# VectorE instead of GpSimd makes the low parts of 72 dense weight pieces in a two-layer decoder trunk

## The chip, the cores and the metric

The kernel runs as one program on one core of a Trainium2 chip. Its time is the device time of one execution in microseconds (us). The engines are named as in the profile: PE is TensorE (PEld its weight loads), DVE is VectorE, ACT is ScalarE, POOL is GpSimd, SP issues most transfers. All of them run side by side, each through its own list of instructions in order, and wait for one another by semaphores.

## The reference

272 tokens (16 meta tokens and 256 of the input) of width 1024 pass two layers. Each layer projects the stream by one matrix of 8192 columns, runs a gated linear recurrence (8 heads) and a causal depthwise convolution of width 31 beside each other, merges both, and ends in a dense SwiGLU (layer 0) or a mixture of 8 experts, two per token (layer 1). Cut to what matters:

```
proj = h @ w_in[l]                                  # Q F I OG CV CG GA GB, 1024 columns each
o = hgrn2_recurrence(proj Q, proj F, proj I)        # per head, chunked over time
y_rec  = (rms_norm(o) * hg_norm_g * silu(proj OG)) @ w_hg_out
u = (proj CV) * sigmoid(proj CG)
y = conv over 31 tokens of u, per channel, + conv_b
y_conv = silu(layer_norm(y)) @ w_conv_out           # mean and variance over all channels
h = layer_norm(ALPHA * h + (sigmoid(proj GA) * y_rec + sigmoid(proj GB) * y_conv) @ w_out)
h = layer_norm(ALPHA * h + swiglu or mixture of experts)
```

## The kernel before

**Split products.** A dense product is made of three TensorE products in the fast float format fp32r: high weight by high input, high weight by low input, low weight by high input. The weights come from memory in pieces of 128 x 1024 numbers (`raw`). For each piece ScalarE copies the high part (`whi`), and then VectorE or GpSimd subtracts it from the piece, which gives the low part (`wlo`); `split` does both. `lo_pool(i)` says which engine makes the low part of piece i: GpSimd for the pieces 0 and 2 to 92 and for 156 to 235, VectorE for the others. A layer's mixer takes 88 pieces (0 to 87 and 156 to 243), the dense SwiGLU of layer 0 the 68 between. `SPLIT` = 6 pieces may stand ready.

**Stages.** The mixer goes through its columns in blocks of 256, two pieces each, in the order CG0 CV0, CG1 CV1, then F I Q of heads 0 to 3, CG2 CV2 CG3 CV3, then F I Q of heads 4 to 7, then the four blocks of OG and the four of GB. Behind those comes the product with `w_conv_out`, whose first two blocks are done together (`gemm_both`, L423) and whose input is the finished, normalised convolution, `yc_hi` and `yc_lo`. The pieces 20 to 55 (and 176 to 211 in layer 1) are those of CG2 up to GB.

**What runs beside.** The convolution (`conv`) is a chain of VectorE instructions: 8 blocks of 128 channels with 31 taps each, 248 taps a layer, each 128x272 (128x256 in layer 1), its input in SBUF and its running sum `st` in PSUM. Then come the sums over channels (`sums`), their TensorE reduction (L650, L651), the inverse deviation (`rstd`, ScalarE) and two passes of VectorE over all blocks. The recurrence (`attention`) runs once for heads 0 to 3 and once for heads 4 to 7: at each span of 1, 2, 4 up to 256 tokens TensorE makes products (L820, L826, L870, L877; bank `ca`), and VectorE multiplies decays into `q`, `k`, `kt` and `c` and copies the products under a mask into `att`. Both are Python generators. Behind each half of a block of weights `gemm` calls `prep`, which writes the splits of the coming pieces, and then `pump`, which takes one step of the recurrence and then as many taps as fit:

```
self.t_dve = max(self.t_dve, self.t_pe - 6.0)
while self.fill and self.t_dve < self.t_pe - 2.0:
    try:
        next(self.fill[0])
```

`t_pe` and `t_dve` are the planner's own counts of TensorE and VectorE work. Every VectorE instruction given out through `self.V` (a `Priced`) adds 0.1 us and its elements per partition / 960 us to `t_dve`; one given out through `nc.gpsimd` adds nothing. Behind the last GB block `finish_fill` writes whatever the convolution has left, with its norm. The order of every engine is fixed by this when the program is built.

Of the kernel before, what the change touches and what calls it, by code (L numbers as in the profile page):

```python
# [48 lines left out]
RAW, SPLIT, DENSE = 6, 6, 244  # L49
# [79 lines left out]
class Trunk:  # L129
# [226 lines left out]
    def lo_pool(self, i):  # L356
        if i >= DENSE:
            return DENSE + 4 <= i < DENSE + 6
        return i != 1 and i < 93 or 156 <= i < DENSE - 8

    def take(self, n):
# [1628 lines left out]
```

## Time and profile before

| | |
|---|---|
| runs | 1883.96, 1885.85, 1886.17 us; median 1885.85 |
| the profiled execution | 1887.53 us, span of the profile 1885.8 us |
| PE busy | 1811.1 us, 96% of the span |
| DVE, ACT, POOL busy | 1068.0 (57%), 824.1 (44%), 483.9 us (26%) |
| GpSimd's low parts | 173 instructions, 418.8 us |
| granted TensorE clock, mean | 0.984 |

Shares over the whole span mix stages. The mixer of layer 0 reaches from about 20 to 360 us, that of layer 1 from about 575 to 925 us, and the mixture of experts fills the time from about 940 us on.

### The profile page before, as it was taken

To read this page: it belongs to the slowest core of one execution; us is meant where nothing else is said; L and a number is where in the kernel's file an instruction comes from. 1 tells how busy PE (TensorE), PEld (TensorE's weight loads), DVE (VectorE), ACT (ScalarE), POOL (GpSimd) and SP (SyncE) were. 2 spreads that over 40 slices of the span, in tenths; PEclk is the share of its full clock that TensorE was granted. 3 is DMA by queue.
4 is the path that set the end of the run, shared out by engine and by line. 5 is a ranking of instruction groups with operands and counts; after the bars stand their busy time and mean duration, and the time that the engine had idled before them with its cause. 6 is when DMAs were issued, how large, how long until landed. Compare 5 with 4: busy or idle time off the path is not lost. (4 is left out here: it accounts for less than half of the span.)

```text
span 1885.8 us, 30795 instructions
## 1 busy us (share of the span) xinstructions
PE 1811.1 (96%) x11577; PEld 1400.9 (74%) x11577; DVE 1068.0 (57%) x1646; ACT 824.1 (44%) x1256; POOL 483.9 (26%) x258
## 2 busy tenths in 40 slices
PE   8989999899999998899899999999999999999996
PEld 7989899799999998899888888887443333433342
DVE  6999834865556899725799998986001001100112
ACT  4635545454446544555487877875001011111111
POOL 6857656500007856654200000000000000000000
PEclk8999999999999999999899999999999999999998
DMA  6534344455554534345689799999999999999995
GB/s 210 172 109 147 100 124 137 132 179 171 180 169 147 169 119 123 112 127 165 221 295 385 277 358 345 360 347 382 393 394 394 394 394 391 395 394 391 378 391 217
DMA packets 284162, 484.88 MB, mean 257 GB/s; under 512 B 15042, under 2 KB 139842, under 8 KB 284006
## 3 DMA queue, kind: packets, MB, share of 16 engines
q1 hardware_dynamic: 283654, 481.75, 72.3%
q8 instruction: 93, 1.52, 0.3%
q0 software_dynamic: 320, 1.08, 0.2%
q14 instruction: 63, 0.52, 0.1%
q10 hardware_dynamic: 32, 0.01, 0.0%
HBM read 481.73 MB, written 1.05 MB: 256 GB/s over the span
## 5 line engine op out<-in xcount | busy, mean ns | idle before, releaser
L126 ACT ACTIVATE whi<-raw 128x1024 fp32r<-128x1024 f32 (+1 forms) x498 | 518.9, 1050 | 113.5 <-PE mm L1565 41.4
L228 POOL TENSOR_TENSOR wlo<-raw,whi 128x1024 fp32r<-128x1024 f32 (+1 forms) x173 | 418.8, 2440 | 375.2 <-ACT whi L126 359.1
L104 DVE TENSOR_TENSOR wlo<-raw,whi 128x1024 fp32r<-128x1024 f32 (+1 forms) x323 | 386.7, 1217 | 92.8 <-ACT whi L126 80.2
L396 PE MATMUL mm<-h_hi,whi 128*128 128x272 f32 (+1 forms) x1280 | 377.7, 295 | 0.9 <-ACT tmp L126 0.9
L398 PE MATMUL mm<-h_hi,wlo 128*128 128x272 f32 (+1 forms) x1280 | 370.4, 289 | 0.0
L397 PE MATMUL mm<-h_lo,whi 128*128 128x272 f32 (+1 forms) x1280 | 369.0, 288 | 0.0
L396 PEld LDWEIGHTS mm<-h_hi,whi 128*128 128x128 f32 x1280 | 243.8, 191 | 2.6 <-ACT tmp L126 1.2
L1900 POOL TENSOR_TENSOR res<-res,four 128x256 f32<-128x256 f32 x2 | 2.3, 1143 | 943.3 <-ACT res L126 943.3
L397 PEld LDWEIGHTS mm<-h_lo,whi 128*128 128x128 f32 x1280 | 244.1, 191 | 0.1
L398 PEld LDWEIGHTS mm<-h_hi,wlo 128*128 128x128 f32 x1280 | 243.4, 190 | 0.0
L1628 PE MATMUL mm<-raw,xg 128*32 128x512 f32 (+1 forms) x896 | 200.6, 604 | 2.3 <-DMA raw<-in_moe_w_gate_dram 1.4
L104 DVE SCALAR_TENSOR_TENSOR st<-wide,cw,st 128x272 f32<-128x272 f32 (+1 forms) x480 | 194.4, 487 | 0.0
L126 ACT ACTIVATE tmp<-mm 128x512 f32<-128x512 f32 (+2 forms) x108 | 54.7, 509 | 245.5 <-PE mm L1628 165.6
L1564 PE MATMUL mm<-whi,xg 128*128 128x512 f32 x336 | 132.7, 395 | 0.0
L1628 PEld LDWEIGHTS mm<-raw,xg 128*32 128x32 f32 (+1 forms) x896 | 57.7, 129 | 99.3 <-issue 70.5
L1565 PE MATMUL mm<-whi,xg 128*128 128x512 f32 x336 | 131.3, 391 | 0.0
L1566 PE MATMUL mm<-wlo,xg 128*128 128x512 f32 x336 | 131.2, 391 | 0.0
L1717 DVE TENSOR_TENSOR tmp<-tmp,ca 128x128 f32<-128x128 f32 x21 | 6.0, 288 | 214.6 <-ACT tmp L126 208.8
L1626 PE MATMUL mm<-raw,xg 128*64 128x256 f32 x896 | 112.4, 388 | 0.8 <-DMA raw<-in_moe_w_up_dram 0.8
L1603 PE MATMUL st<-raw,tmp 128*32 128x512 f32 (+1 forms) x448 | 104.6, 600 | 8.9 <-DMA raw<-in_moe_w_down_dram 7.9
L1626 PEld LDWEIGHTS mm<-raw,xg 128*64 128x64 f32 x896 | 58.6, 137 | 71.1 <-issue 45.6
L126 ACT ACTIVATE tmp<-ca 128x128 f32<-128x128 f32 (+5 forms) x55 | 19.8, 360 | 183.3 <-PE ca L1712 115.9
(356 smaller groups left out, 2868.7 us busy)
## 6 DMA issues: line engine op xcount, KB each, us to landing
raw<-in_moe_w_gate_dram SPq DMA_DIRECT2D x224, 512.0 KB, 10.3
raw<-in_moe_w_up_dram SPq DMA_DIRECT2D x224, 512.0 KB, 10.6
raw<-in_moe_w_down_dram SPq DMA_DIRECT2D x224, 512.0 KB, 10.2
raw<-in_w_in_dram SPq DMA_DIRECT2D x128, 512.0 KB, 3.6
raw<-in_ffn_w_gate_dram SPq DMA_DIRECT2D x22, 512.0 KB, 3.6
raw<-in_ffn_w_up_dram SPq DMA_DIRECT2D x22, 512.0 KB, 3.6
raw<-in_ffn_w_down_dram SPq DMA_DIRECT2D x20, 512.0 KB, 3.4
raw<-in_w_conv_out_dram SPq DMA_DIRECT2D x16, 512.0 KB, 3.4
```

The source lines that it names most:

```text
L104: return f(out, *a, **k)
L126: return self.eng.activation(out, in_, func, **k)
L228: (eng or self.V).tensor_tensor(lo, src, f32(hi), op=ALU.subtract)
L396: nc.tensor.matmul(ps[c], w[i][0][:, a], xh, start=first, stop=False)
L397: nc.tensor.matmul(ps[c], w[i][0][:, a], xl, start=False, stop=False)
L398: nc.tensor.matmul(ps[c], w[i][1][:, a], xh, start=False, stop=last)
L1564: nc.tensor.matmul(bank, x[0](k), whi, start=k == 0, stop=False)
L1565: nc.tensor.matmul(bank, x[1](k), whi, start=False, stop=False)
L1566: nc.tensor.matmul(bank, x[0](k), wlo, start=False, stop=k == KB - 1)
L1603: nc.tensor.matmul(y[c][tile[i % m], :], f(i), w[i - h][:, 0, c * 512:(c + 1) * 512], start=begin and i < m, stop=end and i >= 4 - m)
L1626: nc.tensor.matmul(bank[tile[i], :CW], x(k), v[:, i * CW:(i + 1) * CW], start=k == 0, stop=k == KB - 1)
L1628: nc.tensor.matmul(bank[tile[k % m], :], x(k), v, start=k < m, stop=k >= KB - m)
```

## The change

For the pieces whose number modulo 156 is 20 to 55, that is 20 to 55 of layer 0 and 176 to 211 of layer 1, `lo_pool` now answers no, so that VectorE makes their low parts. No other piece is touched, and no instruction is added or dropped: 36 subtractions in each layer go from GpSimd's list to VectorE's.

```
     def lo_pool(self, i):
         if i >= DENSE:
             return DENSE + 4 <= i < DENSE + 6
+        if i % (DENSE - 88) in range(20, 56):
+            return False
         return i != 1 and i < 93 or 156 <= i < DENSE - 8
```

These 72 subtractions are now counted in `t_dve`, so the planner places the taps anew. VectorE's list of layer 0, from the first two taps of a channel block on, before:

```order
L104 TENSOR_SCALAR st_998<-wide_258,cw_196,cols 128x272
L104 TENSOR_SCALAR st_999<-wide_258,cw_196,cols 128x272
L104 SCALAR_TENSOR_TENSOR st_998<-wide_258,cw_196,st_998 128x272
L104 SCALAR_TENSOR_TENSOR st_999<-wide_258,cw_196,st_999 128x272
L104 SCALAR_TENSOR_TENSOR st_998<-wide_258,cw_196,st_998 128x272
L104 SCALAR_TENSOR_TENSOR st_999<-wide_258,cw_196,st_999 128x272
```

The same place in VectorE's list now (`wlo` of piece 20 and of piece 21):

```order
L104 TENSOR_SCALAR st_998<-wide_258,cw_196,cols 128x272
L104 TENSOR_SCALAR st_999<-wide_258,cw_196,cols 128x272
L104 SCALAR_TENSOR_TENSOR st_998<-wide_258,cw_196,st_998 128x272
L104 SCALAR_TENSOR_TENSOR st_999<-wide_258,cw_196,st_999 128x272
L104 TENSOR_TENSOR wlo_1039<-raw_771,whi_1038 128x1024
L104 SCALAR_TENSOR_TENSOR st_998<-wide_258,cw_196,st_998 128x272
L104 SCALAR_TENSOR_TENSOR st_999<-wide_258,cw_196,st_999 128x272
L104 SCALAR_TENSOR_TENSOR st_998<-wide_258,cw_196,st_998 128x272
L104 SCALAR_TENSOR_TENSOR st_999<-wide_258,cw_196,st_999 128x272
L104 TENSOR_TENSOR wlo_1079<-raw_814,whi_1078 128x1024
```

Here one subtraction stands in front of every four taps. While a recurrence runs, 12 taps stood between two of its steps; now it is two subtractions and 4 to 8 taps.

The end of the convolution in VectorE's list of layer 0, before. Its last tap stands in front of the masked copies of the second recurrence's first span (`att`), and its norm (`sums`, `tmp`) is spread between the following spans:

```order
L104 COPY_PREDICATED att_88<-mask_506,ca_2298 128x4x64
L104 COPY_PREDICATED att_89<-mask_506,ca_2307 64x32
L104 TENSOR_TENSOR sums_262<-sums_262,wide_259 128x272
L104 TENSOR_TENSOR sums_262<-sums_262,tmp_2358 128x272
L104 TENSOR_TENSOR sums_262<-sums_262,wide_259 128x272
L104 TENSOR_TENSOR sums_262<-sums_262,tmp_2363 128x272
L104 TENSOR_TENSOR c_1554<-c_1554 128x544
L104 TENSOR_TENSOR q_1556<-q_1556,c_1554 128x1088
```

The end of the convolution in VectorE's list of layer 0 now, from the last two taps on:

```order
L104 SCALAR_TENSOR_TENSOR st_2500<-wide_259,cw_196,st_2500 128x272
L104 TENSOR_TENSOR sums_262<-sums_262,wide_259 128x272
L104 TENSOR_TENSOR sums_262<-sums_262,tmp_2803 128x272
L104 TENSOR_TENSOR sums_262<-sums_262,wide_259 128x272
L104 TENSOR_TENSOR sums_262<-sums_262,tmp_2808 128x272
L104 TENSOR_TENSOR tmp_2816<-st_2813,tmp_2816 128x272
L104 TENSOR_SCALAR tmp_2816<-tmp_2816 128x272
L104 TENSOR_TENSOR wide_258<-wide_258,st_2812 128x272 x4
L104 TENSOR_TENSOR wide_259<-wide_259,st_2812 128x272 x4
L104 TENSOR_TENSOR wide_258<-wide_258,rstd_2820 128x272 x4
L104 TENSOR_TENSOR wide_259<-wide_259,rstd_2820 128x272 x4
L104 TENSOR_TENSOR q_1516<-q_1516,c_1514 128x4x4x32
```

The last 40 taps of layer 0 (30 of layer 1) now stand behind the second recurrence's step that copies the products of span 16, and the whole norm is one piece behind them. That step is written behind the first half of the last GB block, so these 40 taps, the norm and `yc_hi` all come when TensorE has only that block's second half and the products of span 32 left in front of `gemm_both`; the products of the spans 64, 128 and 256 now stand inside and behind the start of `gemm_both`. Before, the products of 64 and 128 stood in front of it.

## Rows read from the trace of the kernel before

**Rows 1.** Busy time by stretch: start:end, length, PE, PEld, DVE, ACT, POOL, clock, DMA.

```profile
110.00:130.00 20.00, 15.10 (x103) 14.73 (x102) 19.93 (x30) 3.98 (x5) 10.75 (x6) 0.83 0.44 132
700.00:743.00 43.00, 35.45 (x277) 34.61 (x276) 42.57 (x84) 19.77 (x44) 27.19 (x15) 0.92 0.37 111
```

**Rows 2.** Groups of VectorE instructions, 40 to 243 us: busy us, mean ns, idle before.

```profile
L104 DVE TENSOR_TENSOR k<-k,c 128x544 f32<-128x544 f32 x8 | 13.2, 1647 | 0.0
L104 DVE TENSOR_TENSOR k<-k,c 128x512 f32<-128x512 f32 x8 | 9.8, 1227 | 1.1 <-PE ca L870 1.1
...
L104 DVE TENSOR_TENSOR q<-q,c 128x512 f32<-128x512 f32 x6 | 9.3, 1542 | 1.8 <-PE ca L820 1.7
L104 DVE TENSOR_TENSOR q<-q,c 128x544 f32<-128x544 f32 x6 | 8.6, 1440 | 1.5 <-PE ca L826 1.5
```

**Rows 3.** VectorE instructions in order of time: start, length, group, idle before.

```profile
115.95 2.33 DVE L104 TENSOR_TENSOR kt<-kt,c 128x32 f32<-128x32 f32 x1
...
127.55 0.71 DVE L104 TENSOR_TENSOR k<-k,c 128x544 f32<-128x544 f32 x1
128.19 0.18 DVE L104 TENSOR_TENSOR kt<-kt,c 128x32 f32<-128x32 f32 x1
...
137.41 4.98 DVE L104 SCALAR_TENSOR_TENSOR st<-wide,cw,st 128x272 f32<-128x272 f32 x12
```

**Rows 4.** GpSimd instructions in order of time, the same stretch.

```profile
107.87 12.66 POOL L228 TENSOR_TENSOR wlo<-raw,whi 128x1024 fp32r<-128x1024 f32 x5
```

**Rows 5.** Groups of VectorE instructions, 380 to 560 us, where GpSimd is idle.

```profile
L104 DVE TENSOR_TENSOR wlo<-raw,whi 128x1024 fp32r<-128x1024 f32 x59 | 73.5, 1249 | 58.6 <-ACT whi L126 58.5
```

**Rows 6.** What TensorE waited for, 90 to 243 us: total, times, longest.

```profile
PE ca L826 <- DVE att L104: 5.0, 2, 4.2
PE ca L820 <- DVE k L104: 4.5, 3, 2.8
```

**Rows 7.** What TensorE waited for, 640 to 800 us.

```profile
PE ca L870 <- DVE k L104: 4.4, 2, 2.8
PE ca L820 <- DVE k L104: 3.4, 3, 1.4
PE ca L826 <- DVE att L104: 3.0, 2, 1.5
PE ca L877 <- DVE k L104: 2.7, 1, 2.7
```

**Rows 8.** TensorE in order of time, around the last GB block of layer 0.

```profile
228.74 1.49 PE L820 MATMUL ca<-q,k 128*96 128x64 f32 x16
...
236.06 1.55 PE L820 MATMUL ca<-q,k 128*64 128x64 f32 x16 [2.75 <-DVE k L104]
...
242.64 0.50 PE L423 MATMUL mm<-yc_hi,whi 128*128 128x272 f32 x2
```

**Rows 9.** The same of layer 1.

```profile
787.48 1.49 PE L820 MATMUL ca<-q,k 128*96 128x64 f32 x16
...
798.84 1.13 PE L870 MATMUL ca<-q,k 128*128 128x128 f32 x8 [1.61 <-DVE k L104]
799.72 0.48 PE L423 MATMUL mm<-yc_hi,whi 128*128 128x256 f32 x2
```

**Rows 10.** All engines in order of time, from the last taps of layer 0 to `yc_hi`.

```profile
183.27 2.53 DVE L104 SCALAR_TENSOR_TENSOR st<-wide,cw,st 128x272 f32<-128x272 f32 x6
...
186.61 0.43 ACT L126 ACTIVATE tmp<-wide 128x272 f32<-128x272 f32 x1
...
202.24 0.62 PE L651 MATMUL st<-sums,ones 128*128 128x272 f32 x2
...
206.90 2.55 DVE L104 TENSOR_TENSOR wide<-wide,st 128x272 f32<-128x272 f32 x7
...
220.22 0.61 ACT L126 ACTIVATE wide<-wide,cols 128x272 f32<-128x272 f32 x1 [4.75 <-DVE wide L104]
220.87 0.43 ACT L126 ACTIVATE yc_hi<-wide 128x272 fp32r<-128x272 f32 x1
```

More of the change, by code (lines that the diff above doesn't have):

```diff
@@ L358, in lo_pool @@
             return DENSE + 4 <= i < DENSE + 6
+        if i % (DENSE - 88) in range(20, 56):
+            return False
         return i != 1 and i < 93 or 156 <= i < DENSE - 8
```

## The prediction

> **What bounds the kernel now.** Over the whole span TensorE is busy 96% of the time, so only what lets TensorE stop less, or makes it stop more, changes the total. I read first the busy time by stretch, to find where it stops. It runs full through the dense SwiGLU and most of the experts; it stops in the two mixers. In layer 0 from 110 to 130 us it works 15.1 of 20 us while VectorE works 19.93, and in layer 1 from 700 to 743 us it works 35.45 of 43 us while VectorE works 42.57 [rows 1]. There VectorE is the engine that ends last. The waits of TensorE say the same by name: in layer 0 all 9.5 us are waits for VectorE's `att` and `k` [rows 6], in layer 1 so are all 13.5 us shown [rows 7]. The clock falls with the stops: it is granted at 0.83 and at 0.92 of full speed in these stretches [rows 1], that is in part at 1.2 instead of 2.4 GHz.
>
> Then I read why VectorE is full, in its own order of time. The same instruction on `kt`, 32 numbers per partition, takes 2.33 us at 115.95 and 0.18 us at 128.19 [rows 3]. At the first of these GpSimd works through five low parts in one run, 107.87 to 120.5 us, 2.53 us each [rows 4]; the second falls behind that run. A VectorE product of two SBUF tensors is thus held while a GpSimd subtraction runs. The groups carry it through the layer: 8 instructions on `k` of 544 numbers take 1647 ns on the mean instead of 0.71 us, and 8 on `k` of 512, 6 on `q` of 512 and 6 on `q` of 544 take 1.2 to 1.5 us instead of about 0.7 [rows 2, 3]. Four groups take 13.2 + 9.8 + 9.3 + 8.6 = 40.9 us for 28 instructions that would need about 28 x 0.7 = 19.6. So 21 us are waiting, and with `kt` (6 instructions) and the small `c` I estimate 27 us in each layer. The taps don't suffer: 12 take 4.98 us at 137.41 [rows 3], 0.415 us each, with GpSimd at work beside them.
>
> The Trainium skill, page "SBUF — State Buffer", section "Who interferes with whom", has the rule for both: a VectorE instruction with two SBUF inputs contends with a GpSimd instruction that reads SBUF, one with a single SBUF input does not. The trace agrees (2.33 against 0.18 us; taps unchanged). The Trainium skill's page "Perfetto Trace Analysis", section "Optimizing Scalar/DVE Operations", speaks against the change: it has a saturated VectorE give work away, to ScalarE or even GpSimd, though it warns that the shared port may eat the gain. By that rule the outcome is rival A below.
>
> **What the change costs VectorE.** 36 subtractions a layer. Where GpSimd is idle, one takes 1.249 us on VectorE [rows 5], so 45 us are added to each layer. Of the 27 us of waiting nearly all goes, since GpSimd then has only sums in that stretch; it keeps the pieces from 56 on, which are due when the last two GB blocks run. Net some 18 us more on an engine that had nothing to spare. But the planner counts the new instructions (1.17 us each against 1.249), while it never counted the waiting (0.67 us for a `k` that took 1.65). It answers by putting taps off: 40 taps of layer 0 (16.6 us) and 30 of layer 1 now come after the step of span 16. So I don't expect TensorE to stop at each span; the load that is too much collects at one place, in front of `gemm_both`.
>
> **The end of the convolution (the loss).** The clock of this sum starts when TensorE begins the last GB block, behind the products of span 32 in the old order: 228.74 + 1.49 = 230.2 us; `gemm_both` starts at 242.64 [rows 8]. That is 12.4 us. In the new order VectorE's step of span 16 can't start before that point, for it overwrites what the products of span 16 read. It needs two products of 0.7 us, a small one and two masked copies, together 2.4 us (an estimate from the same rows); GpSimd makes the pieces 56 to 59 just then, so each of the three products may be held as in [rows 3], up to 7 us more. I take 3.5. Then 40 taps of 0.415, 16.6. Then the norm, which can't hide behind anything as TensorE's list has nothing else in front: copies and squares 1.2 (last tap ends at 185.80, last square at 187.04), one more sum 0.4, two pairs of reductions of about 0.6, 1.2; two short VectorE steps, about 0.8; eight subtractions, 2.55 x 8/7 = 2.9; one product with `rstd`, 0.4; ScalarE 0.61 + 0.43 [rows 10]. Sum 7.9. So `yc_hi` stands 3.5 + 16.6 + 7.9 = 28.0 us behind that point, 15.6 later than before. The products of 64 and 128 (1.55 + 1.13 [rows 8, 9]) now come behind the start of `gemm_both`, but those of 32 and the reductions (1.49 + 1.2) fall into TensorE's stop; these cancel.
>
> In layer 1 the same point is 787.48 + 1.49 = 789.0, and `gemm_both` starts at 799.72 [rows 9]: 10.7 us. New: 3.5 + 30 x 0.40 (a tap is 256 wide there) + 7.9 = 23.4, so 12.7 later. TensorE then stands some 20 us in layer 0 and 15 in layer 1. After the stops of 110 to 130 us it lost 0.17 x 20 = 3.4 us to the lower clock, part of it while it stood anyway [rows 1]; I take 2 us for each layer. Loss: 15.6 + 12.7 + 4 = 32.3 us. Bounds: 26 (no hold by GpSimd, no clock) and 42 (5 us of hold more in each).
>
> **The stops that go (the gain).** Stops in front of that point: layer 0 9.5 - 2.75 (the one at 236.06 lies behind it) = 6.8 us [rows 6, 8]; layer 1 13.5 - 1.6 - about 1.1 = 10.8 us [rows 7, 9]. Clock: 3.4 us from 110 to 130 and 0.08 x 43 = 3.4 from 700 to 743, half of it on time counted already, so 3.5. In all 21 us if every one goes. The lower bound is none, as VectorE stays nearly full. I take 70%, 14.7 us, nearer to the upper end because the long stops come where GpSimd's runs hold VectorE for several instructions in a row, and those runs vanish.
>
> GpSimd's saved 36 x 2.5 us a layer are worth nothing by themselves: nothing else waits for it there. ScalarE's high parts and SP's loads keep their number and kind. What lies behind the mixers is full of TensorE or transfers, so a delay passes through.
>
> **Sum.** -14.7 + 32.3 = +17.6 us. The profiled execution took 1887.5 us (span 1885.8), 1.7 us above the median of the runs, so in terms of the median 1885.85 + 17.6 = 1903.5; I say 1903.
>
> **Rivals.**
> A, VectorE can't keep up. If the waiting doesn't go away (it would have another cause than GpSimd), 45 us a layer fall on an engine that is idle 0.07 of 20 and 0.43 of 43 us [rows 1]: 1885.85 + 90 = 1975. For it: VectorE is full. Against it: 2.33 against 0.18 us. Chance 0.04.
> B, nothing comes back. VectorE is as late at each span as before, now through its own subtractions, and the end is as priced, held by GpSimd or not: +32 to +42, 1918 to 1928. For it: its load stays at nearly all of the time. Against it: the planner now counts what loads it. Chance 0.15.
> C, faster: VectorE's own sum decides. `yc_hi` starts at 220.87 [rows 10]; with 45 us more and 27 us less it would be ready at 238.9, 3.8 us ahead of 242.64, so the end would cost nothing, and both layers would gain as much, 1878. It decides if VectorE is never held by TensorE on the way, above all not at the step of span 16: that needs TensorE to be there some 9 us earlier than priced. Against it: TensorE can come only as much earlier as its stops give back, 6.8 us in layer 0, all of which I have already counted. Chance 0.09.
> That the change doesn't do what it says is out: the order shows the 72 moves.
>
> **How the numbers follow.** The forecast's own case, stops mostly gone and the end as priced, has 0.72 and reaches from +5 (26 - 21) to +25 us, 1891 to 1911. The measurement can tell 0.2%, 3.8 us. Below 1882.1 lies C: faster 0.09. Between lie the forecast's best corner and a part of C: same 0.08. All else, slower 0.83. The range leaves out A, C and the upper part of B: 1890 to 1922.
>
> **What would show it.** Right: `kt`, `k` and `q` at their short times from 95 us on; the waits of TensorE for `k` and `att` in mid-stage mostly gone; and one stop in front of `gemm_both`, about 20 us in layer 0 and 15 in layer 1, whose releaser is ScalarE's `yc_hi`, with a fall of the clock behind it. Wrong: stops at every span (A or B), or VectorE through its last tap while TensorE is still in GB (C). The forecast fails most easily in the share of stops that go, and in how far GpSimd's pieces 56 to 59 hold the steps of the last two blocks.

## The result and the profile after

The changed kernel took 1898.89 us in the median of four runs (1895.56 to 1903.87), beside 1885.89 for four runs of the kernel before on the same chip. The ratio is 1.0076, with a 95% interval of 1.0058 to 1.0093; on 1885.85 us that is 14.3 us slower. The profiled execution is the slowest of the four: 1903.87 us, with a span of 1902.2 against 1885.8.

Busy time by stretch in the changed kernel (columns as in [rows 1]); the first two stretches answer to those rows, the others are the middle of layer 0's mixer and its end:

```profile
110.00:130.00 20.00, 20.00 (x163) 19.78 (x163) 19.26 (x39) 7.01 (x11) 0.00 (x0) 1.00 0.54 156
700.00:743.00 43.00, 42.71 (x366) 42.27 (x366) 38.00 (x74) 23.50 (x49) 0.24 (x1) 1.00 0.47 138
...
92.00:216.00 124.00, 123.99 (x1009) 122.31 (x1009) 116.60 (x220) 50.62 (x90) 9.89 (x11) 1.00 0.45 135
216.00:248.00 32.00, 12.15 (x92) 11.00 (x91) 29.80 (x74) 9.19 (x16) 6.60 (x3) 0.71 0.19 60
```

TensorE, which worked 15.10 of 20 us in the first stretch, now works all of it, and 123.99 of 124 us through the middle of the mixer, at full clock. All that is lost stands in one place: from 216 to 248 us it works 12.15 of 32 us.

Groups of VectorE instructions, 40 to 248 us (columns as in [rows 2]):

```profile
L104 DVE TENSOR_TENSOR wlo<-raw,whi 128x1024 fp32r<-128x1024 f32 x36 | 44.1, 1224 | 7.6 <-ACT whi L126 7.6
...
L104 DVE TENSOR_TENSOR q<-q,c 128x544 f32<-128x544 f32 x6 | 6.1, 1016 | 0.6 <-PE ca L828 0.6
L104 DVE TENSOR_TENSOR k<-k,c 128x544 f32<-128x544 f32 x8 | 5.7, 718 | 0.0
...
L104 DVE TENSOR_TENSOR kt<-kt,c 128x32 f32<-128x32 f32 x6 | 1.1, 185 | 0.0
```

The 36 subtractions cost 44.1 us. The products that GpSimd held are short: `k` 718 ns instead of 1647, and no `kt` above 0.2 us. `q` stays at 1016 ns on the mean, because single ones still meet a subtraction of GpSimd's (pieces from 56 on).

What TensorE waited for, 90 to 290 us and then 660 to 860 us (columns as in [rows 6]; lines behind the edit are two higher than before):

```profile
PE st L652 <- DVE sums L104: 14.7, 1, 14.7
PE mm L425 <- ACT yc_hi L126: 5.2, 1, 5.2
PE ca L872 <- DVE k L104: 2.4, 1, 2.4
PE mm L425 <- POOL yc_lo L228: 1.9, 1, 1.9
...
PE st L652 <- DVE sums L104: 10.5, 1, 10.5
PE mm L425 <- ACT yc_hi L126: 5.0, 1, 5.0
PE ca L879 <- DVE k L104: 0.3, 1, 0.3
```

The waits for `k` and `att` of [rows 6, 7] are gone. In their place stands one stop in each layer in two pieces, around TensorE's reductions (L652, L653). The order of time shows what fills it. VectorE, then all engines:

```profile
219.82 1.57 DVE L104 TENSOR_TENSOR q<-q,c 128x512 f32<-128x512 f32 x1
...
222.17 0.76 DVE L104 COPY_PREDICATED att<-mask,ca 112x256 f32<-112x256 uint8 x2
222.83 16.42 DVE L104 SCALAR_TENSOR_TENSOR st<-wide,cw,st 128x272 f32<-128x272 f32 x40
...
246.45 2.90 DVE L104 TENSOR_TENSOR wide<-wide,rstd 128x272 f32<-128x272 f32 x8
```

```profile
240.69 1.28 PE L652 MATMUL st<-sums,ones 128*128 128x272 f32 x2 [14.72 <-DVE sums L104]
...
247.57 0.43 ACT L126 ACTIVATE yc_hi<-wide 128x272 fp32r<-128x272 f32 x1
...
248.05 0.82 PE L425 MATMUL mm<-yc_hi,whi 128*128 128x272 f32 x2 [5.18 <-ACT yc_hi L126]
248.07 3.10 POOL L228 TENSOR_TENSOR yc_lo<-wide,yc_hi 128x272 fp32r<-128x272 f32 x1 [22.62 <-ACT yc_hi L126]
```

The 40 taps that the planner put off run from 222.83 to 239.25 us with TensorE idle; then come the norm, `yc_hi` and `gemm_both`.

Two stretches of each mixer carry the whole difference: A, from the first product of span 1 of heads 0 to 3 to the first product of `gemm_both`, and B, from there to the first product with `w_hg_out`. Their ends are read from TensorE's order of time. The time between the layers' stretches (337 to 341 us) and behind the last one (1024 to 1028) is the same in all these kernels, but for one named below.

| kernel | layer 0: A, B | layer 1: A, B |
|---|---|---|
| before | 151.9, 63.7 | 154.8, 60.7 |
| changed | 157.8, 75.1 | 149.7, 64.9 |

### The profile page after: what moved, and what is told of

Its sections match the earlier page's. It is cut to its first block, busy times and chain, and to the rows that moved or that the text cites. A ratio compares the mean times of both kernels' runs of the same rounds, so it can differ in the third digit from the quotient of the medians.

```text
span 1902.2 us, 30769 instructions
## 1 busy us (share of the span) xinstructions
PE 1811.8 (95%) x11577; PEld 1400.3 (74%) x11577; DVE 1093.6 (57%) x1718; ACT 825.0 (43%) x1256; POOL 303.5 (16%) x186
## 3 DMA queue, kind: packets, MB, share of 16 engines
HBM read 481.73 MB, written 1.05 MB: 254 GB/s over the span
## 5 line engine op out<-in xcount | busy, mean ns | idle before, releaser
L104 DVE TENSOR_TENSOR wlo<-raw,whi 128x1024 fp32r<-128x1024 f32 (+1 forms) x395 | 474.6, 1218 | 111.8 <-ACT whi L126 99.2
L228 POOL TENSOR_TENSOR wlo<-raw,whi 128x1024 fp32r<-128x1024 f32 (+1 forms) x101 | 242.0, 2415 | 321.7 <-ACT whi L126 319.2
## 6 DMA issues: line engine op xcount, KB each, us to landing
raw<-in_moe_w_up_dram SPq DMA_DIRECT2D x224, 512.0 KB, 10.5
```

The source lines that it names most:

```text
L104: return f(out, *a, **k)
L228: (eng or self.V).tensor_tensor(lo, src, f32(hi), op=ALU.subtract)
```

## The experiments

Eleven kernels ran, in three groups, each beside 17 runs of the kernel before on the same chip (medians 1885.3, 1885.8 and 1884.2 us, single runs 1876 to 1889). Ratios are to those.

**One layer at a time.** `lo_pool` answers no for the pieces of one layer only.

```
+        if i in range(20, 56):          # only_layer0
+        if i in range(176, 212):        # only_layer1
```

> The change in layer 0 alone (pieces 20 to 55); layer 1 as before. The prediction's own terms give layer 0 +15.6 + 2 us of loss and 70% of 8.55 us of gain: +11.6 us, about 1897.5 us. The trace of the changed kernel gives more: its second mixer starts 17.15 us later than before, so if the layers add up, about 1903 us. If the loss lies evenly in both layers, +6.5 us, about 1892 us.

> The change in layer 1 alone (pieces 176 to 211); layer 0 as before. The prediction's own terms give 12.7 + 2 us of loss and 70% of 12.55 us of gain: +5.9 us, about 1891.8 us. The trace of the changed kernel says that layer 1 gains: from the start of its second mixer to the first product behind gemm_both it is 3.7 us shorter than before, so about 1882 us. If the loss lies evenly in both layers, about 1892 us.

Layer 0 alone: 1897.86 us, ratio 1.0069 (1.0048 to 1.0090), 13 us. Layer 1 alone: 1886.91 us, ratio 1.0010 (0.9997 to 1.0024), no difference that can be told. Their sum is the change. Layer 0 came out near the prediction's own share (+11.6), layer 1 below it (+5.9). By the trace of the changed kernel alone I had read 17 and -4. The layer that was left alone shows how far one execution can be trusted: A of layer 0 is 147.0 us in this execution of the kernel with layer 1 alone, and 151.9 in that of before, with the same instructions.

**The subtractions uncounted.** All 72 on VectorE, but the planner doesn't count them, so taps and norm stand as before.

```
             eng = self.nc.gpsimd if self.lo_pool(i) else self.V
+            if i < DENSE and i % (DENSE - 88) in range(20, 56):
+                eng = self.nc.vector
```

> All 72 low parts on VectorE, but given out without being counted in t_dve, so that the planner places taps and norm as before. Theory 1 (the cost is the putting off of taps to the place in front of gemm_both): no stop of 15 us there, the norm is ready ahead of gemm_both, and what is left is VectorE's 18 us more of work a layer, spread over the spans: 1875 to 1890 us, clearly below the changed kernel's 1899. Theory 2 (the cost is VectorE's load itself, wherever the taps stand): TensorE waits for k and att at each span for what is lacking, 18 us a layer less some 6 of spare time, so 1910 us or more.

1923.69 us, ratio 1.0209 (1.0185 to 1.0233): slower than the changed kernel by 25 us. What TensorE waited for, 88 to 330 us:

```profile
PE ca L824 <- DVE k L104: 13.1, 5, 5.6
PE ca L874 <- DVE k L104: 3.1, 2, 1.7
PE ca L824 <- DVE kt L104: 1.6, 1, 1.6
```

The stop in front of `gemm_both` is gone, and B is as before (63.7 and 60.7 us); instead TensorE waits at nearly every span, and A is 173.5 and 170.4 us. So the second theory holds here: the load doesn't go away when the taps are not put off. The putting off is not a mistake of the planner's; it made the loss smaller.

**Neither engine makes the low parts.** ScalarE does, as a copy, once with the taps of before and once with those of the changed kernel.

```
+                    if i < DENSE and i % (DENSE - 88) in range(20, 56):
+                        self.A.activation(hi[:, c], t[:, c], AF.Copy)
+                        self.A.activation(lo[:, c], t[:, c], AF.Copy)      # scalar_lows_counted: scale=0.0
+                        self.t_dve += 0.1 + m / 960.0                      # scalar_lows_counted only
```

> The 72 low parts are made by ScalarE as a plain copy of the piece, so the low parts' numbers are left out of the result; neither GpSimd nor VectorE has that work, and the planner's order is that of before. It prices the gain alone. If every stop in front of the last GB block goes: 1885.85 - 21 by the prediction's count, about 1865 us; by the trace of the changed kernel, in which the last GB block starts 11.7 us earlier in layer 0 and 19.1 us earlier in layer 1, down to 1855. If only 70% of the stops were due to GpSimd: about 1871. If the stops had another cause: about 1886.

> ScalarE fills the 72 low parts with zeros (a copy with scale 0, so the low parts' share is left out of the result), and the planner still counts 1.17 us for each: the changed kernel's order of taps with neither GpSimd's nor VectorE's subtractions. It prices the putting off alone. Theory 1 (a tap behind the last GB block costs what it takes, whoever makes the low parts): against the same kernel uncounted, whose mixers took 10.0 and 17.5 us less than before, each layer loses what the prediction summed, 15.6 + 12.7 + 4 = 32.3 us, so 1885.85 - 27.5 + 32.3 = about 1891 us, with one stop of 10 to 20 us in front of gemm_both. Theory 2 (the order costs nothing by itself, VectorE's load does): about 1858 us.

The first took 2148.18 us, but that says nothing: TensorE makes 12725 products instead of 11577, and the part behind layer 1's mixer takes 1316 us instead of 1025. I put that down to other tokens going to other experts with the changed numbers. Its mixers can be read: A and B are 142.0 and 63.7, 137.3 and 60.7 us, that is 10.0 and 17.5 us below the profiled execution of before. That is all that GpSimd's holds cost in that execution, 27.5 us.

The second took 1895.34 us, ratio 1.0068 (1.0049 to 1.0088), like the changed kernel. Its stops, 88 to 330 us and 630 to 900 us, and its middle stretch:

```profile
PE st L657 <- DVE sums L104: 14.7, 1, 14.7
PE mm L430 <- ACT yc_hi L126: 5.2, 1, 5.2
...
PE st L657 <- DVE sums L104: 10.5, 1, 10.5
PE mm L430 <- ACT yc_hi L126: 5.0, 1, 5.0
```

```profile
92.00:216.00 124.00, 124.00 (x1013) 122.71 (x1012) 80.08 (x180) 78.46 (x120) 10.24 (x11) 1.00 0.44 135
```

VectorE works 80.08 us in the stretch where it worked 116.60 in the changed kernel, and the stops are the same to a tenth. So, within the scatter of the runs (the two intervals overlap), the changed kernel's time is set by its order alone, by the taps that stand behind the step of span 16. VectorE's 44 us of subtractions a layer cost nothing by themselves in that order; their cost is that the taps had to give way. Against scalar_lows, the same edit without the counting, the order costs (157.3 + 67.5) - (142.0 + 63.7) = 19.1 us in layer 0 and (148.9 + 64.9) - (137.3 + 60.7) = 15.8 in layer 1, about 35 together, by one execution of each.

**The pieces that hold, and as many others.** In the trace of before I took for each of GpSimd's subtractions the time that VectorE's products beside it lasted beyond their shortest; 23.9 us in layer 0 and 30.4 in layer 1 over the pieces of the change, most of it beside 10 and 14 of the 36. One kernel moves the holding pieces (with 56 or 57 to 59, 14 and 17 in all), the other as many that hold nothing or little. The holds beside the first add up to 28.5 and 33.7 us; the 29.4 and 34.3 below are a slip of mine.

```
             eng = self.nc.gpsimd if self.lo_pool(i) else self.V
+            if i in HELD:
+                eng = self.nc.vector
```

> The kernel before, but VectorE makes only those low parts beside which GpSimd held a VectorE product for over 1.25 us in the trace of before (14 pieces in layer 0 and 17 in layer 1, pieces 57 to 59 of each among them), uncounted, so with the taps of before. The held time beside them adds up to 29.4 and 34.3 us, their cost on VectorE is 14 and 17 times 1.25 us, 17.5 and 21.3. Theory 1 (VectorE's net sum decides, and the holds stay where the trace has them): 12 to 13 us less on VectorE in each layer, of which half to all comes back: 1862 to 1876 us. Theory 2 (the pieces that GpSimd keeps move up and hold other products instead): cost without relief, 17 to 21 us a layer, 1910 to 1925 us. In between: 1886.

> As the run with the held pieces, with as many others (14 and 17) beside which the trace of before shows no held product or one below 1.25 us. Theory 1 (net sum): their cost, 17.5 and 21.3 us, comes with nothing back: 1905 to 1925 us. Theory 2 (only the number of subtractions counts, since the holds move): the same time as the run with the held pieces, within 4 us.

1890.30 us, ratio 1.0030 (1.0017 to 1.0044), and 1916.46 us, ratio 1.0168 (1.0152 to 1.0185). Which pieces are moved makes 26 us of difference, so the number alone is not it. But the holding ones bring no gain either; the result lies in between. VectorE, a TensorE product and, last, GpSimd in the kernel that moves the holding pieces:

```profile
123.24 2.38 DVE L105 TENSOR_TENSOR kt<-kt,c 128x32 f32<-128x32 f32 x1
125.66 2.47 DVE L105 TENSOR_TENSOR c<-c 128x136 f32<-128x136 f32 x1
...
225.58 1.22 DVE L229 TENSOR_TENSOR wlo<-raw,whi 128x1024 fp32r<-128x1024 f32 x1 [6.69 <-ACT whi L127]
```

```profile
228.23 3.22 PE L823 MATMUL ca<-q,k 128*112 128x64 f32 x16 [7.69 <-DVE k L105]
```

```profile
121.99 5.88 POOL L229 TENSOR_TENSOR wlo<-raw,whi 128x1024 fp32r<-128x1024 f32 x2 [11.72 <-ACT whi L127]
```

Two of the pieces that stayed with GpSimd now run at 121.99 and hold `kt` and `c`: the holds have moved. And a subtraction in VectorE's list brings a wait of its own, 6.69 us for ScalarE's high part, with the `q` and `k` of the next span queued behind it; TensorE's wait for that `k` is 7.7 us.

**The clock behind the stop.** Products of ones, which nothing reads, in TensorE's stops of the changed kernel.

```
+        self.warm((46, 30)[l])
         self.finish_fill()
+        self.warm((18, 13)[l])
```

> The changed kernel with products of ones by ones in TensorE's stops in front of gemm_both (46 and 18 in layer 0, 30 and 13 in layer 1), which nothing reads. It prices the clock behind the stop. In the changed kernel the two reductions took 2.2 us at half clock against 1.2, and the first 24 products of gemm_both 8.08 and 5.14 us (1.9 of the first a wait) against 3.25 and 3.11. If the clock stays up: 1 + 2.9 + 1 + 2.0 = 6.9 us less, about 1892. If the lower clock lies on time that TensorE would have waited anyway, or the added products make the reductions late: 1898 or more.

1893.91 us, ratio 1.0051 (1.0038 to 1.0064), 4.7 us below the changed kernel's by the ratios, with intervals that overlap. TensorE in order of time:

```profile
240.78 1.28 PE L652 MATMUL st<-sums,ones 128*128 128x272 f32 x2 [4.40 <-DVE sums L104]
...
242.76 4.63 PE L181 MATMUL ca<-ones 128*128 128x128 f32 x36
...
252.90 1.12 PE L822 MATMUL ca<-q,k 128*64 128x64 f32 x16 [1.03 <-DVE k L104]
```

The first 24 products of `gemm_both` take 3.7 us; in two kernels of the same order without the added ones they take 4.8 and 4.9. But then TensorE waits 1.03 us for `k`, and B is 67.4 us, as in those two (67.4 and 67.5). So in these executions most of what the clock gave back was waited again. The 6.9 us of the expectation mixed the clock with a wait of the profiled execution; neither case came out clean.

**Other work for TensorE.** The four GA blocks, which need neither the convolution nor VectorE, go in front of `finish_fill` and `gemm_both`; the weights are loaded in that order.

```
-            order = ... all4("OG", "GB", "CO", "GA", "HO", "WO")
+            order = ... all4("OG", "GB", "GA", "CO", "HO", "WO")
...
+        o = []
+        self.stream.append(self.heads(l, sog, o, t0, n))
+        ga = self.halves(n, nm="ga")
+        ge = to(ga, AF.Copy)
+        for j in range(4):
+            self.gemm(h, t0, n, lambda i, ps, j=j: ge(i, ps, j))
         self.finish_fill()
```

The same lines are taken out behind the `w_conv_out` blocks. gates_first has this on the changed kernel, gates_first_np the norm's three pauses taken out as well, gates_first_b has it on the kernel before.

> The changed kernel with the four GA blocks (and the heads' generator) put in front of finish_fill and gemm_both instead of behind the w_conv_out blocks, weights loaded in that order: 25 to 26 us of TensorE work a layer that needs neither the convolution nor VectorE. Nothing is left out. Theory 1 (the cost of the change is that TensorE has no other work while VectorE does the taps that were put off): the taps are done under GA, the stops of 14.7 + 7.1 and 10.5 + 5.0 us shrink to the norm's chain of 8 us or less, and with the clock some 20 to 30 us come back: 1868 to 1880 us, below both kernels. Theory 2 (VectorE's load decides, wherever TensorE's work stands): the stops move behind GA and 1895 us or more stays.

> As the run with GA in front, and the three pauses of the convolution's norm are taken out of the planner, so that the norm is written out under GA too. Theory 1: no stop is left in front of gemm_both, and the time comes near to the mixers without any of the 36 low parts (27.5 us less than before): 1858 to 1868 us. Theory 2: 1895 us or more. A rival to the first: VectorE waits for TensorE's reductions inside the norm and makes the heads late, 1870 to 1880.

> The kernel before (GpSimd makes the low parts) with the GA blocks put in front in the same way, the control. Its convolution was ready ahead of gemm_both already, and its stops are VectorE's held steps in mid-stage: by theory 1 nothing to gain there, 1882 to 1890 us. If it falls as far as the run with the change, the order alone is the gain and the place of the low parts has no part in it.

1873.32 us, ratio 0.9933 (0.9920 to 0.9946); 1868.81 us, ratio 0.9913 (0.9900 to 0.9927); and 1884.35 us, ratio 0.9992 (0.9980 to 1.0003). The place where the taps stood in the way, in the first and in the second of them, and TensorE's waits from 40 to 330 us in the second:

```profile
216.00:248.00 32.00, 32.00 (x274) 31.78 (x272) 29.16 (x66) 15.63 (x29) 21.45 (x10) 1.00 0.47 151
216.00:248.00 32.00, 30.40 (x253) 29.80 (x253) 30.87 (x72) 15.43 (x29) 18.44 (x8) 1.00 0.48 149
```

```profile
PE mm L398 <- DVE tmp L104: 2.7, 1, 2.7
PE ca L920 <- ACT tmp L126: 1.9, 1, 1.9
PE st L652 <- DVE sums L104: 1.6, 1, 1.6
...
PE mm L425 <- ACT yc_hi L126: 0.8, 1, 0.8
```

VectorE is as full there as in the changed kernel, 29.16 and 30.87 of 32 us beside 29.80, with the same 40 taps; TensorE now works 32.00 and 30.40 of 32 beside it instead of 12.15. The order alone gains nothing on the kernel before, and the change alone loses; together (gates_first) they are 13 us faster than the kernel before and 27 us faster than the changed kernel. The first run and the one on the kernel before came inside their expected ranges. With the pauses out as well it is 16 and 31 us; that run lies between the ranges of its two cases, and it has no control of its own, since the kernel before was not run with the pauses out.

## Why the prediction was right, point by point

**Direction and size.** Forecast 1903 us, 17.6 slower; measured 1898.89, 14.3 slower by the ratio. The case is the forecast's own. The gain was 12.3 us larger than taken, and the loss by 4 us in any execution and by 11 in the profiled one. That the total came so near is in part luck: these errors have opposite signs.

**The waiting goes with GpSimd's subtractions.** Right: `k` from 1647 to 718 ns, `kt` at 185 ns. The 27 us of waiting estimated for each layer were near it: beside the pieces of the change the trace of before has 23.9 and 30.4.

**No stop at each span; the load collects in front of `gemm_both`.** Right, and shown from three sides: TensorE 123.99 of 124 us in the middle, the same stops with ScalarE's low parts in the same order, stops at the spans again when the taps are not put off. One reason has to be put more exactly. I spoke of the taps put off as the loss; the uncounted kernel shows that they are the cheaper of two forms of VectorE's load.

**The share of the stops that goes, 70% of 21 us.** This is the term that was most mis-sized: all went, and they were worth more than I had counted. From the first product of span 1 to the start of the last GB block, layer 0 took 230.04 - 90.72 = 139.3 us before and 218.31 - 90.27 = 128.0 after; layer 1 788.78 - 644.87 = 143.9 and 786.98 - 662.02 = 125.0. That is 11.3 + 18.9 us, but not all of it is stops: the products of span 32 and the norm's two reductions stand behind this point now. What both are worth can be read from scalar_lows (ScalarE's copies with the taps of before), which has the order of before and, like the changed kernel, hardly a stop of TensorE in the same stretch. First before, then changed, then scalar_lows (columns as in [rows 1]):

```profile
90.72:230.04 139.32, 132.59 (x1067) 130.64 (x1066) 130.58 (x249) 64.17 (x117) 91.96 (x48) 0.98 0.40 122
644.87:788.78 143.91, 131.99 (x1068) 129.70 (x1066) 125.51 (x227) 67.72 (x126) 92.68 (x50) 0.96 0.39 118
...
90.27:218.31 128.04, 128.03 (x1047) 126.36 (x1046) 120.64 (x228) 53.42 (x94) 11.71 (x11) 1.00 0.46 136
662.02:786.98 124.96, 124.67 (x1047) 123.06 (x1046) 117.73 (x226) 56.50 (x102) 11.13 (x11) 1.00 0.46 140
...
90.12:220.00 129.88, 129.88 (x1068) 128.42 (x1066) 107.72 (x248) 93.53 (x149) 17.64 (x19) 1.00 0.42 127
633.75:760.12 126.37, 126.37 (x1067) 124.97 (x1066) 96.17 (x225) 95.46 (x156) 14.56 (x19) 1.00 0.44 132
```

The moved products are worth 129.88 - 128.04 = 1.8 us in layer 0 and 1.4 in layer 1. So 27.0 us came back, against 14.7 taken and 21 as the upper bound, and nothing was left to come back. TensorE's idle time in this stretch was 6.7 + 11.9 us before, near the 6.8 + 10.8 that I had named; the other 8 us are products that took longer, at a granted clock of 0.98 and 0.96, for which I had taken 3.5. So the share should have been all, and the clock more than twice what I gave it. The bound was too low since I summed the named waits of two windows and half of the clock that the two stretches of [rows 1] showed.

**The end of the convolution.** Step by step in layer 0, from the start of the last GB block at 218.31: the step of span 16 was through at 222.83, 4.5 us (3.5 taken; VectorE came to it 1.5 us late); 40 taps 16.4 (16.6); the norm to `gemm_both` at 248.05, 8.8 (7.9). Sum 29.7 against 28.0. In layer 1 4.5, 11.8 and 8.4 give 24.8 against 23.4. With the 12.4 and 10.7 us of before, 17.3 + 14.1 = 31.4 us instead of 28.3. The mechanism and its parts hold.

**The products that move, and the clock.** The products of 64 and 128 take 1.14 + 1.05 us inside `gemm_both`; less the 1.8 and 1.4 us of span 32 and the reductions that fell into the stop, the moves cost 0.4 and 0.8 us where I let them cancel. B grew by 4.2 us in layer 1, and in layer 0 by 3.7 and 3.8 in two other executions of this order; less 2.2 for the moved products, 1.5 to 2.0 us are left for the clock, as the 2 us a layer had it. In the profiled execution B of layer 0 grew by 11.4, 7.6 more than elsewhere (last section). The sum for that execution is -27.0 + 31.4 + 1.2 + 3.5 + 7.6 = +16.7 us, and its span grew by 16.4; without the 7.6 it is +9.1, about where the fastest run (1895.56) lies. The median stands between.

**What would show it.** The stop's first releaser is VectorE's `sums`, which I had not named: TensorE's two reductions stand in front of `gemm_both` and split the stop, 14.7 + 5.2 us and 10.5 + 5.0. Its length, about 20 and 15, is as forecast. The fall of the clock is there too.

**The rivals.** A (the waiting has another cause) and B (nothing comes back) fall with the middle stretch. C (VectorE's own sum decides) fails as forecast, though a figure of the argument against it was too low: 9.4 us of stops came back in layer 0 where it allowed 6.8. TensorE comes 11.3 us earlier to the last block, but the taps stand behind the step that waits for it. VectorE's 7.6 us of waiting for ScalarE's `whi`, in front of its own subtractions, stood in no sum; the kernel whose VectorE has none of them stops for the same time, so this cost nothing here.

The Trainium skill, page "Perfetto Trace Analysis", section "Optimizing Scalar/DVE Operations", stood against the change: it has a saturated VectorE give work away. By itself the change bears that out (1.0076). But with GA in front it is the kernel whose VectorE has the more work that gains: ratio 0.9933, where the same order with the work left on GpSimd gives 0.9992.

## What to carry to other kernels

When work is moved onto a full engine, ask what gives way and where that ends: a planner that counts the new work moves the excess to the end of the stage, one that doesn't spreads it over every step, and neither time is that of the moved instructions. Look then for work of the waiting engine that doesn't depend on the late result and put it there; only with that did the relief of the shared access become time. A stop that vanishes is worth more than its named waits, since half-clock products and waits of other names go with it.

## What the runs showed that was not expected

The hold works both ways, and small shifts in time decide who holds whom. In the profiled execution of the changed kernel GpSimd's first `yc_lo` takes 3.10 us beside a row of VectorE products that stay short, where two of them take 1.67 us in the kernel with layer 0 alone. There TensorE's products of span 64 started at 252.67 us, here at 256.06, and VectorE's next step with them. First VectorE in the changed kernel, then in the kernel with layer 0 alone; the low parts of GpSimd's next run begin at 257.20 and 257.09 us:

```profile
257.44 2.69 DVE L104 TENSOR_TENSOR q<-q,c 128x512 f32<-128x512 f32 x1 [6.23 <-PE ca L822]
260.06 2.84 DVE L104 TENSOR_TENSOR k<-k,c 128x512 f32<-128x512 f32 x1
```

```profile
253.84 1.24 DVE L104 TENSOR_TENSOR q<-q,c 128x512 f32<-128x512 f32 x1 [0.65 <-PE ca L822]
255.00 1.15 DVE L104 TENSOR_TENSOR k<-k,c 128x512 f32<-128x512 f32 x1
```

In the one the step meets the run and each product lasts over 2.6 us, in the other it is through before. With the waits that follow, B is 75.1 against 67.4 us, for the same instructions in layer 0. The Trainium skill, page "SBUF — State Buffer", section "Who interferes with whom", calls the access that VectorE and GpSimd share an exclusive lock, and has issue order decide who blocks; the trace agrees, and shows besides that a row of VectorE products keeps GpSimd out for longer than one of them (3.10 us beside products of 0.7). I hold such meetings for the reason of the 8 us spread of the changed kernel's runs; that was not tried by itself.
